# Store queue, start order and weight rows of a gMLP and attention layer

## The chip, the cores and the metric

The kernel runs on one core of one Trainium2 chip. A core has five engines that run at the same time, each with its own list of instructions that it takes in order: TensorE (PE, matmuls and transposes into PSUM), VectorE (DVE), ScalarE (ACT), GpSimd (POOL) and SyncE (SP), which here only issues DMAs. The weight load of a matmul has a row of its own in the profile (PEld). Engines wait for each other through semaphores. The metric is the device time of one execution, in microseconds.

## The reference

One layer over a sequence of 1024 rows with 1024 features, all in float32:

```python
h = rms_norm(x, g_pre)
proj = h @ w_in            # u_A, v_A, z_A, q, k, v_B, z_B, two gates
y_a = spatial_gating(gelu(u_a), gelu(v_a), ln_g, ln_b, w_s, b_s) * silu(z_a)
y_b = mixture_of_dilations(q, k, v_b) * silu(z_b)     # 8 heads of 128
m = g_a * (y_a @ w_pa) + g_b * (y_b @ w_pb)
return x + rms_norm(m @ w_o, g_post)
```

spatial_gating normalises v_A and mixes the 128 rows of each chunk by a 128x128 matrix w_s of each of 16 groups; its bias b_s is added to what w_s makes of ln_b. mixture_of_dilations lets each query see a window of keys at three strides, with a bias that falls with the distance, and combines the three results by their softmax denominators.

## The kernel before

**Products.** Every float32 operand is split in two parts, hi (a rounded copy, made on ScalarE) and lo (the difference, on VectorE or GpSimd); a product is three matmuls: hi by hi, hi by lo and lo by hi. `operand` (L98 to L109) does that for a weight tile and `split` (L159) for an activation.

**Order.** Loops emit the work; a scheduler then sets each engine's list by its own estimate of times and by the order of emission. `tc.issue_after(i)` keeps what is emitted inside it behind instruction i in that order. Pools with few buffers add waits: raw weight tiles and the tiles of y_A share the tag `wr` with three buffers, hi and lo operands have eight each (`wh`, `wl`), PSUM tags have one to three banks. SP issues its DMAs in list order, so a store that waits for its data holds all behind it.

**Start (to 150 us).** Eight row tiles of x are loaded. For each, `norm_tile` squares it on ScalarE (L253), takes the root as a power on GpSimd (L164), scales it by its root and by g_pre on VectorE (L260) and transposes it on TensorE in `transposed` (L241), with the split behind. Meanwhile `warm` (L229) runs idle matmuls. The first weight operands are those of the v_B projection, `vb`, in row pairs. `rows_product` (L148 to L156) runs that projection in passes over eight k; the table in the loop below it names what is emitted ahead of which k (`ahead`): the norm of a further tile, sums of tiles (`sum_tile`), or `spatial_weights(q)` for four groups of w_s. The latter loads w_s, fills two rows of `shift` with a memset (L301) and a DMA, transposes on TensorE (L306), copies and splits, then makes row sums (`wsR`, L313), copies them with VectorE (L314), multiplies them by ln_b and b_s (`wsB`, L318), copies the product and stores it.

**Projections (150 to 1023 us).** All other columns of w_in by a scheme of seven block products. The change leaves them alone.

**Heads (1023 to 1350 us).** `queries_keys` loads q, k (krh, krl) and the distance tables (ta, te, tb) of a head; `residue_values` and `chunk_values` load its values, the latter in 16 small DMAs (L661, L662); `scores` runs the score matmuls (L702 to L704), the add of a table with a row maximum on VectorE (L707) and the exponential on ScalarE (L711); `exchange` (L715 to L724) moves row sums between the patterns, `normalise` (L728 to L742) makes one factor of them, `scale` (L747 to L761) applies it; `weigh` transposes the weights (L779), multiplies them by the values (L798, L813), adds and gates the result (L865, L866) and stores it to o_d (L867). Beside the heads runs the product y_A @ w_pa: `mlp_weights` loads raw tiles of w_pa and yields operands, two tiles of y_A rows (`yf`) at a time come by `mlp_tiles`, and `mlp_products` runs one step of three matmuls (one k) for each `take(steps, 1)`. In names, pa0110 is b 0, m 1, half 1, part 0.

**Tail.** o_d is loaded again, then the products with w_pb (L1046 to L1048) and w_out, the last norm and the output.

## Time and profile before

| | |
|---|---|
| median of 3 runs | 1560.0 us (1558.48 to 1561.28) |
| profiled execution | 1557.3 us |
| its span | 1555.5 us |
| mean granted TensorE clock | 0.991 |
| TensorE busy | 1509.7 us, 97% of the span |
| VectorE, ScalarE, GpSimd busy | 871.0, 683.6, 780.2 us |
| DMA moved | 251.64 MB, 162 GB/s over the span |

The span runs from the first to the last instruction of the profiled execution. A row of a timeline gives start, duration, engine, line, operation, and in brackets how long the engine had been idle before it and what ended that. A row of waits gives who waited for whom: microseconds in all, how many times, the longest. "from issue to landing" is the last number of a DMA row.

### The profile page before, as it was taken

How to read it: one execution, taken by the hardware profiler on the slowest of the kernel's cores; microseconds unless marked ns; L12 is line 12 of the kernel's file. 1: busy time of each engine (PE TensorE's matmuls, PEld its weight loads, DVE VectorE, ACT ScalarE, POOL GpSimd, SP SyncE). 2: the span in 40 equal slices, each digit the busy share in tenths (PEclk: the TensorE clock that was granted, in tenths of full speed). 3: DMA queues.
4: the chain of work that ended last, by engine and by line, in shares of the span. 5: the costliest groups of instructions: out<-in, count | busy, mean ns of one | idle time of the engine just before them, and what ended most of it. 6: DMA issues, size and time to landing. Idle time of an engine off the chain costs nothing.

```text
span 1555.5 us, 22766 instructions
## 1 busy us (share of the span) xinstructions
PE 1509.7 (97%) x7866; PEld 1274.4 (82%) x7866; DVE 871.0 (56%) x1699; ACT 683.6 (44%) x1318; POOL 780.2 (50%) x711
## 2 busy tenths in 40 slices
PE   8999999999999999999999999998999989999998
PEld 5788999988788888788888888877887778878886
...
GB/s 250 158 156 192 140 109 103 107 129 132 171 120 142 135 166 103 164 127 138 154 112 153 105 173 113 128 240 256 202 223 203 224 209 186 247 273 166 185 109 68
DMA packets 247798, 251.64 MB, mean 162 GB/s; under 512 B 14297, under 2 KB 187385, under 8 KB 247426
## 3 DMA queue, kind: packets, MB, share of 16 engines
...
q8 instruction: 62, 1.02, 0.3%
q14 instruction: 54, 0.44, 0.1%
...
HBM read 173.58 MB, written 76.55 MB: 161 GB/s over the span
## 4 chain that ended last, share of the span: by engine, by line
PE 75%; DVE 9%; issue 5%; ACT 4%; DMA 3%; POOL 3%; SPq 0%; POOLq 0%; DVEq 0%; ACTq 0%
PE pa L921 2%; PE pa L922 2%; PE pa L923 2%; PE pb L1047 2%; PE pb L1048 2%; PE pb L1046 2%; PE vb L154 2%; PE vb L155 2%; PE vb L156 2%; PE sg L567 2%; ACT st L711 1%; POOL out L1067 1%; PE pc L813 1%; DVE oth L724 1%; PE pr L798 1%
## 5 line engine op out<-in xcount | busy, mean ns | idle before, releaser
L108 POOL TENSOR_TENSOR wl_pa<-wr_pa,wh_pa 128x512 fp32r<-128x512 f32 x56 | 74.6, 1342 | 42.7 <-ACT wh_pa L106 34.1
L556 DVE TENSOR_SCALAR vn<-vn,mean,rstd 128x128 f32<-128x128 f32 x128 | 58.4, 510 | 35.8 <-DMA vn<-v_d 35.4
L711 ACT ACTIVATE st<-st,own 128x256 f32<-128x256 f32 (+1 forms) x128 | 62.7, 494 | 35.1 <-DVE own L707 35.0
L1046 PE MATMUL pb<-yh,wh_pb 128*128 128x512 f32 x128 | 49.9, 390 | 1.4 <-ACT yh L159 1.4
L106 ACT ACTIVATE wh_pa<-wr_pa 128x512 fp32r<-128x512 f32 x64 | 38.8, 624 | 27.5 <-DMA wr_pa<-in_w_proj_a_dram 18.9
L1047 PE MATMUL pb<-yl,wh_pb 128*128 128x512 f32 x128 | 50.0, 391 | 0.7 <-DVE yl L159 0.5
L1048 PE MATMUL pb<-yh,wl_pb 128*128 128x512 f32 x128 | 49.8, 389 | 0.0
L724 DVE COPY oth<-own 32x4 f32<-32x4 f32 x128 | 36.0, 281 | 15.0 <-ACT st L711 13.4
L1081 ACT ACTIVATE sq<-o 128x512 f32<-128x512 f32 x16 | 9.6, 599 | 74.6 <-PE o L1079 74.6
L159 POOL TENSOR_TENSOR qcl<-q,qch 128x512 fp32r<-128x512 f32 x16 | 27.8, 1739 | 28.1 <-ACT qch L159 28.1
L159 POOL TENSOR_TENSOR vl<-vn,vh 128x512 fp32r<-128x512 f32 x32 | 41.3, 1292 | 0.8 <-ACT vh L159 0.8
L1050 POOL TENSOR_TENSOR mb<-thb,mb 128x512 f32<-128x512 f32 x16 | 20.6, 1289 | 41.7 <-DVE thb L1049 32.2
L724 POOL COPY oth<-own 32x4 f32<-32x4 f32 x128 | 24.0, 188 | 31.6 <-ACT st L711 26.8
L1061 DVE TENSOR_TENSOR sso<-sso 128x1 f32<-128x1 f32 x8 | 1.3, 160 | 67.6 <-ACT sq L1081 67.6
L759 DVE TENSOR_SCALAR st<-st,nm 128x256 f32<-128x256 f32 x64 | 36.9, 619 | 0.3
L164 POOL TENSOR_TENSOR sso<-sso,mhalf 128x1 f32<-128x1 f32 x8 | 4.4, 550 | 59.1 <-DVE sso L163 59.1
L159 DVE TENSOR_TENSOR ptlb<-pb,pthb 128x512 fp32r<-128x512 f32 x32 | 22.0, 688 | 20.2 <-ACT pthb L159 20.2
L866 POOL TENSOR_TENSOR o<-o,zt 128x512 f32<-128x512 f32 x16 | 20.6, 1295 | 24.5 <-DMA zt<-z_d 13.3
L108 POOL TENSOR_TENSOR wl_wos<-wr_wos,wh_wos 128x512 fp32r<-128x512 f32 x16 | 20.7, 1292 | 22.8 <-ACT wh_wos L106 22.8
L707 DVE CUSTOM_DVE_ANT_0 st<-sc,tb 128x256 f32<-128x256 f32 x64 | 23.6, 420 | 14.3 <-PE sc L704 12.9
L779 PE MATMUL pb<-ident,st 128*128 128x128 f32 x128 | 21.2, 286 | 9.5 <-DVE st L759 6.8
L1046 PEld LDWEIGHTS pb<-yh,wh_pb 128*128 128x128 f32 x128 | 24.0, 188 | 6.7 <-ACT yh L159 1.8
...
## 6 DMA issues: line engine op xcount, KB each, us to landing
wr_pa<-in_w_proj_a_dram SPq DMA_DIRECT2D x32, 512.0 KB, 5.7
wr_g<-in_w_in_dram SPq DMA_DIRECT2D x16, 512.0 KB, 3.5
wr_va<-in_w_in_dram SPq DMA_DIRECT2D x16, 512.0 KB, 3.7
wr_u<-in_w_in_dram SPq DMA_DIRECT2D x16, 512.0 KB, 3.7
wr_z<-in_w_in_dram SPq DMA_DIRECT2D x16, 512.0 KB, 3.7
...
wr_yf<-y_d SPq DMA_DIRECT2D x16, 512.0 KB, 5.8
```

What stands on the lines that cost most here:

```text
L106: nc.scalar.activation(hi, src, AF.Copy)
L108: low.tensor_tensor(lo, src, f32(hi), ALU.subtract)
L154: nc.tensor.matmul(ps, lhs[k][0], rh, start=(k == 0), stop=False)
L155: nc.tensor.matmul(ps, lhs[k][0], rl, start=False, stop=False)
L159: return nc.scalar.activation(hi, src, AF.Copy), low.tensor_tensor(lo, src, f32(hi), ALU.subtract)
L556: nc.vector.tensor_scalar(vn[:, c, :], vn[:, c, :], mean[:, 4 * b + c, 0:1], rstd[:, 4 * b + c:4 * b + c + 1], op0=ALU.subtract, op1=ALU.mult)
L711: nc.scalar.activation(st[:, t, :n], st[:, t, :n], AF.Exp, bias=own[:, half, idx, 0:1], scale=-1.0, accum_out=own[:, half, idx, 1:2])
L724: (nc.gpsimd, nc.vector)[half].tensor_copy(dst, src)
L759: nc.vector.tensor_scalar(w, w, f, None, op0=ALU.mult)
L1046: nc.tensor.matmul(ps, lh, rh, start=(k == 0), stop=False)
L1047: nc.tensor.matmul(ps, lh, rl, start=False, stop=False)
L1048: nc.tensor.matmul(ps, ll, rh, start=False, stop=(k == KT - 1))
```

## The change

1. **First rows.** `transposed` also returns the low split, `norm_tile` also the scale. `spatial_weights` is emitted behind tile 0's last transpose and its low split, the first weight operands behind tile 0's scale.
2. **Spatial bias.** The part of `spatial_weights` from wsB on is returned as a function and emitted one step later in the table, behind the newest matmul of `rows_product`.
3. **Stores.** The outputs of the heads go to o_d by GpSimd's queue and no longer by SP's.
4. **Weight rows.** A raw tile of w_pa holds 4 k-blocks of 256 columns (rows of 1 KB) in place of 8 k-blocks of 128 columns. Two such tiles make the operands of two m. There are 32 loads of 512 KB as before.
5. **Chunk values of head 0** are emitted behind `queries_keys(1)` and no longer ahead of head 0's scores.

```diff
@@ -153,7 +153,9 @@
             for ps, lhs in zip(pss, lhss):
                 nc.tensor.matmul(ps, lhs[k][0], rh, start=(k == 0), stop=False)
                 nc.tensor.matmul(ps, lhs[k][0], rl, start=False, stop=False)
-                nc.tensor.matmul(ps, lhs[k][1], rh, start=False, stop=(k == KT - 1))
+                newest[:] = [nc.tensor.matmul(ps, lhs[k][1], rh, start=False, stop=(k == KT - 1))]
+
+    newest = []
 
     def split(hi, lo, src, low=nc.vector):
         return nc.scalar.activation(hi, src, AF.Copy), low.tensor_tensor(lo, src, f32(hi), ALU.subtract)
@@ -239,8 +241,7 @@
             pt = bank("pv", name)
             for k in range(4):
                 last = nc.tensor.transpose(pt[:, k * P:(k + 1) * P], src[:, k * P:(k + 1) * P], ident)
-            split(*[t[:, :, i * P:(i + 1) * P] for t in hl], pt.rearrange("p (k n) -> p k n", k=4))
-            return last
+            return last, split(*[t[:, :, i * P:(i + 1) * P] for t in hl], pt.rearrange("p (k n) -> p k n", k=4))[1]
 
         def norm_tile(c, load=1, between=None):
             b, i = divmod(c, 4)
@@ -257,10 +258,10 @@
             power(ss[:, 1:2], ss[:, 0:1], 1.0 / D)
             for j in range(2):
                 xs = xt[:, 512 * j:512 * (j + 1)]
-                nc.vector.scalar_tensor_tensor(xs, xs, ss[:, 1:2], gpre[:, 512 * j:512 * (j + 1)], op0=ALU.mult,
+                scaled = nc.vector.scalar_tensor_tensor(xs, xs, ss[:, 1:2], gpre[:, 512 * j:512 * (j + 1)], op0=ALU.mult,
                                                op1=ALU.mult)
                 last = transposed(hT[j][b], i, xs, f"xT{c}{j}")
-            return squared, last
+            return squared, scaled, last
 
         def v_out(c, cb, ps):
             if cb:
@@ -312,26 +313,30 @@
             pr_ = bank("sc", f"wsR{q}")
             nc.tensor.matmul(pr_[0:1, :], col, wf, start=True, stop=True)
             nc.vector.tensor_copy(rowsum[0:1, :], pr_[0:1, :])
-            pb = bank("sc", f"wsB{q}")
-            for g in range(4):
-                gs = slice(g * P, (g + 1) * P)
-                nc.tensor.matmul(pb[:, gs], shift[0:2, gs], rowsum[0:2, gs], start=True, stop=True)
-            wb = wpool.tile([P, 512], F32, tag="ws", bufs=2, name=f"wb{q}")
-            nc.scalar.activation(wb, pb, AF.Copy)
-            nc.sync.dma_start(wsb_d[q].rearrange("p g n -> p (g n)"), wb)
+
+            def biases():
+                pb = bank("sc", f"wsB{q}")
+                for g in range(4):
+                    gs = slice(g * P, (g + 1) * P)
+                    nc.tensor.matmul(pb[:, gs], shift[0:2, gs], rowsum[0:2, gs], start=True, stop=True)
+                wb = wpool.tile([P, 512], F32, tag="ws", bufs=2, name=f"wb{q}")
+                nc.scalar.activation(wb, pb, AF.Copy)
+                nc.sync.dma_start(wsb_d[q].rearrange("p g n -> p (g n)"), wb)
+
+            return biases
 
         def norm_weights(squared):
             for j, pg in enumerate(spread):
                 with tc.issue_after(squared.ins):
                     nc.scalar.activation(gpre[:, 512 * j:512 * (j + 1)], pg, AF.Copy)
 
-        squared, turned = norm_tile(0, 0, norm_weights)
+        squared, scaled, turned = norm_tile(0, 0, norm_weights)
         rows = sp.tile([32, P], F32, name="rows")
         wv = []
         for k in range(0, KT, 2):
             if k == 2:
                 norm_tile(4, 0)
-            with tc.issue_after(squared.ins):
+            with tc.issue_after(squared.ins), tc.issue_after(scaled.ins):
                 wv += row_pair(w_in, OFF_VB, k, "vb0", (nc.gpsimd, nc.vector) if k < 4 else (nc.gpsimd, nc.gpsimd))
             if k == 0:
                 load_tile()
@@ -343,14 +348,28 @@
 
         def spatial(q):
             def emit():
-                with tc.issue_after(turned.ins), tc.issue_after(squared.ins):
-                    spatial_weights(q)
+                with tc.issue_after(turned[0].ins), tc.issue_after(turned[1].ins), tc.issue_after(squared.ins):
+                    after[q] = spatial_weights(q)
             return emit
 
+        def bias(q):
+            def emit():
+                with tc.issue_after(newest[0].ins):
+                    after[q]()
+            return emit
+
+        def both(*fs):
+            def emit():
+                for f in fs:
+                    f()
+            return emit
+
+        after = {}
+
         norm, sums = (lambda c, n=1: lambda: norm_tile(c, n)), (lambda i: lambda: sum_tile(i))
-        for cb, cs, tags, ahead in ((0, (0, 4), "mm mm", {1: spatial(0), 2: norm(1), 3: spatial(1), 4: spatial(2), 5: norm(5),
-                                                          6: spatial(3)}),
-                                    (0, (1, 5), "sc sc", {0: norm(2), 2: sums(0), 3: norm(6), 5: sums(1), 6: norm(3), 7: norm(7, 0)}),
+        for cb, cs, tags, ahead in ((0, (0, 4), "mm mm", {1: spatial(0), 2: norm(1), 3: both(bias(0), spatial(1)), 4: both(bias(1), spatial(2)),
+                                                          5: norm(5), 6: both(bias(2), spatial(3))}),
+                                    (0, (1, 5), "sc sc", {0: norm(2), 1: bias(3), 2: sums(0), 3: norm(6), 5: sums(1), 6: norm(3), 7: norm(7, 0)}),
                                     (0, (2, 6, 3, 7), "sc tp mm mm", {3: sums(2)}),
                                     (1, (0, 4, 1, 5), "sc sc sc tp", {3: sums(3)}),
                                     (1, (2, 6, 3, 7), "mm mm sc sc", {})):
@@ -864,7 +883,7 @@
                 o4 = o[:, hs].rearrange("p (a i r) -> p a i r", a=4, r=4)
                 nc.vector.tensor_tensor(o4, po[b].rearrange("p (a r i) -> p a i r", a=4, r=4), o4, ALU.add)
                 nc.gpsimd.tensor_tensor(o[:, hs], o[:, hs], zs[b], ALU.mult)
-                nc.sync.dma_start(o_d[h][:, hs], o[:, hs])
+                nc.gpsimd.dma_start(o_d[h][:, hs], o[:, hs])
             yield
 
 
@@ -888,11 +907,11 @@
 
         def mlp_weights():
             for b, p, half in MLP_ORDER:
-                for m in (2 * p, 2 * p + 1):
-                    raw = raw_tile(w_pa[8 * half * P:8 * (half + 1) * P, m * P:(m + 1) * P].rearrange(
-                        "(k p) n -> p k n", p=P), f"pa{b}{m}{half}")
+                raw = [raw_tile(w_pa[4 * q * P:4 * (q + 1) * P, 2 * p * P:2 * (p + 1) * P].rearrange(
+                    "(k p) n -> p k n", p=P), f"pa{b}{p}{q}") for q in (2 * half, 2 * half + 1)]
+                for m in range(2):
                     for g in range(2):
-                        yield operand(raw[:, 4 * g:4 * g + 4, :], f"pa{b}{m}{half}{g}",
+                        yield operand(raw[g][:, :, m * P:(m + 1) * P], f"pa{b}{2 * p + m}{half}{g}",
                                       nc.vector if (b, p) == (0, 0) else nc.gpsimd)
 
         def mlp_products(ya):
@@ -937,7 +956,6 @@
         take(queries_keys(0, heads[0]))
         take(steps, 8)
         residue_values(0, heads[0])
-        chunk_values(0, heads[0])
         for _ in scores(0, heads[0]):
             take(steps, 1)
         take(exchange(0, heads[0], 0))
@@ -947,6 +965,7 @@
             scale(heads[0], *tile_)
         for _ in queries_keys(1, heads[1]):
             take(steps, 3)
+        chunk_values(0, heads[0])
         before = iter(())
         for h in range(H):
             more = h + 1 < H
```

**What moves at the start.** VectorE, between tile 0's root and the first low split. ss_149 is of tile 0 and ss_187 of tile 4, the second to be worked on; xt_120 is tile 0. Before:

```order
L163 TENSOR_SCALAR ss0_149<-ss0_149,eps_74 128x1
L301 MEMSET shift0_253 2x512
L301 MEMSET shift1_321 2x512
L260 SCALAR_TENSOR_TENSOR xt0_120<-xt0_120,ss0_149,gpre_122 128x512 x2
L108 TENSOR_TENSOR wl_vb0_1_183<-wr_vb0_0_175,wh_vb0_1_181 128x512
L256 TENSOR_TENSOR ss4_187<-ss4_187 128x1
L159 TENSOR_TENSOR hT00l_101<-xT00_159,hT00h_100 128x4x128
L163 TENSOR_SCALAR ss4_187<-ss4_187,eps_74 128x1
```

and now:

```order
L165 TENSOR_SCALAR ss0_149<-ss0_149,eps_74 128x1
L261 SCALAR_TENSOR_TENSOR xt0_120<-xt0_120,ss0_149,gpre_122 128x512 x2
L108 TENSOR_TENSOR wl_vb0_1_183<-wr_vb0_0_175,wh_vb0_1_181 128x512
L257 TENSOR_TENSOR ss4_187<-ss4_187 128x1
L165 TENSOR_SCALAR ss4_187<-ss4_187,eps_74 128x1
L161 TENSOR_TENSOR hT00l_101<-xT00_159,hT00h_100 128x4x128
```

Both memsets of shift have moved behind tile 4's scale, and tile 4's ss stands ahead of hT00l.

TensorE, at the last group of spatial weights (q is 3, the digit behind ws); vb01 are the accumulators of the second pass. Before:

```order
L313 MATMUL wsR3_445<-wf3_428,col_147 1x512
L318 MATMUL wsB3_448<-rowsum3_427,shift3_426 128x128 x4
L154 MATMUL vb01_0_480<-wh_vb0_0_177,hT00h_100 128x512
L155 MATMUL vb01_0_480<-wl_vb0_0_179,hT00h_100 128x512
L156 MATMUL vb01_0_480<-wh_vb0_0_177,hT00l_101 128x512
```

and now:

```order
L314 MATMUL wsR3_445<-wf3_428,col_147 1x512
L154 MATMUL vb01_0_472<-wh_vb0_0_177,hT00h_100 128x512
L155 MATMUL vb01_0_472<-wl_vb0_0_179,hT00h_100 128x512
L156 MATMUL vb01_0_472<-wh_vb0_0_177,hT00l_101 128x512
L154 MATMUL vb01_1_473<-wh_vb0_0_177,hT01h_102 128x512
L155 MATMUL vb01_1_473<-wl_vb0_0_179,hT01h_102 128x512
L156 MATMUL vb01_1_473<-wh_vb0_0_177,hT01l_103 128x512
L154 MATMUL vb01_0_472<-wh_vb0_1_181,hT00h_100 128x512
L155 MATMUL vb01_0_472<-wl_vb0_1_183,hT00h_100 128x512
L321 MATMUL wsB3_505<-rowsum3_427,shift3_426 128x128 x4
```

Eight matmuls of the second pass have come between the row sums and the product that uses them.

**What moves at head 0.** ScalarE, at the exponentials of its scores: st0 are score tiles (st010 of the strided half, st003 of the plain one), wh_pa operand copies of w_pa, ya0201h the copies of the y_A rows that are loaded as yf020 and yf022, qrh1 and qch1 the next head's queries. Before:

```order
L711 ACTIVATE st010_9836,own0_9834<-st010_9836,own0_9834 128x256
L711 ACTIVATE st012_9852,own0_9834<-st012_9852,own0_9834 128x256 x2
L711 ACTIVATE st014_9873,own0_9834<-st014_9873,own0_9834 128x256 x2
L711 ACTIVATE st016_9888,own0_9834<-st016_9888,own0_9834 128x256 x2
L711 ACTIVATE st001_9909,own0_9834<-st001_9909,own0_9834 128x256
L106 ACTIVATE wh_pa0200_9802<-wr_pa020_9800 128x512
L106 ACTIVATE wh_pa0201_9902<-wr_pa020_9800 128x512
L711 ACTIVATE st001_9909,own0_9834<-st001_9909,own0_9834 128x256
L711 ACTIVATE st003_9924,own0_9834<-st003_9924,own0_9834 128x256 x2
L711 ACTIVATE st005_9943,own0_9834<-st005_9943,own0_9834 128x256 x2
L711 ACTIVATE st000_9958,own0_9834<-st000_9958,own0_9834 128x192 x2
```

and now:

```order
L730 ACTIVATE st001_9891,own0_9816<-st001_9891,own0_9816 128x256 x2
L106 ACTIVATE wh_pa0011_9751<-wr_pa003_9745 128x512
L106 ACTIVATE wh_pa0110_9755<-wr_pa002_9743 128x512
L106 ACTIVATE wh_pa0111_9778<-wr_pa003_9745 128x512
L161 ACTIVATE ya0201h_9766<-wr_yf020_9768 128x512 x2
L730 ACTIVATE st003_9906,own0_9816<-st003_9906,own0_9816 128x256 x2
L730 ACTIVATE st005_9925,own0_9816<-st005_9925,own0_9816 128x256 x2
L161 ACTIVATE qrh1_10014<-q10_10020 128x4x128
L161 ACTIVATE qch1_10016<-q10_10020 128x512
L730 ACTIVATE st000_9940,own0_9816<-st000_9940,own0_9816 128x192
L161 ACTIVATE ya0201h_9766<-wr_yf022_9790 128x512 x2
L730 ACTIVATE st000_9940,own0_9816<-st000_9940,own0_9816 128x192
```

The exponentials now stand among copies of four operands and of y_A rows, and the last of them behind the copies of yf022.

**What moves at head 5.** SP, around its keys; ve and va are the values of head 4, ma_d the store of a finished tile of y_A @ w_pa, tha06 its data. Before:

```order
L635 DMA krh5_11829<-k_d_90 128x1024
L113 DMA wr_yf110_11951<-y_d_94 128x2x512
L635 DMA krl5_11830<-k_d_90 128x1024
L639 DMA ta5_12003<-in_alibi_a_dram 128x256
L928 DMA ma_d_95<-tha06_11808 128x512
L639 DMA te5_12005<-in_alibi_e_dram 128x384
L662 DMA ve04_11983<-vb_h_84 16x2x128 x4
L662 DMA ve14_11993<-vb_l_85 16x2x128 x4
L639 DMA tb5_12007<-in_alibi_b_dram 128x384
```

and now:

```order
L654 DMA krh5_11829<-k_d_90 128x1024
L113 DMA wr_yf110_11953<-y_d_94 128x2x512
L947 DMA ma_d_95<-tha06_11808 128x512
L681 DMA ve04_11985<-vb_h_84 16x2x128 x4
L681 DMA ve14_11995<-vb_l_85 16x2x128 x4
L654 DMA krl5_11830<-k_d_90 128x1024
L680 DMA va14_11994<-vb_l_85 32x7x128
L680 DMA va04_11984<-vb_h_84 32x7x128 x4
L680 DMA va14_11994<-vb_l_85 32x7x128 x3
L658 DMA ta5_12005<-in_alibi_a_dram 128x256
L658 DMA te5_12007<-in_alibi_e_dram 128x384
L658 DMA tb5_12009<-in_alibi_b_dram 128x384
```

The low keys have moved behind the store and eight small loads, the tables behind another eight.

## The prediction, made before the result was known

> **What bounds the kernel now.** I read the page's busy times first, then the windows by stage, then the timelines and waits of the stages that are not full.
>
> ```profile
> PE 1509.7 (97%) x7866; PEld 1274.4 (82%) x7866; DVE 871.0 (56%) x1699; ACT 683.6 (44%) x1318; POOL 780.2 (50%) x711
> 0.00:20.00 20.00, 15.85 (x43) 7.65 (x43) 9.80 (x21) 10.10 (x21) 7.64 (x12) 1.00 0.64 224
> 20.00:40.00 20.00, 19.48 (x98) 12.74 (x99) 13.71 (x28) 13.89 (x32) 4.55 (x6) 1.00 0.90 276
> 40.00:60.00 20.00, 17.23 (x90) 13.15 (x90) 13.84 (x25) 10.03 (x24) 7.56 (x7) 0.91 0.58 186
> 500.00:600.00 100.00, 100.00 (x456) 82.92 (x455) 63.08 (x97) 39.23 (x64) 54.48 (x41) 1.00 0.44 140
> 1025.00:1060.00 35.00, 28.70 (x140) 22.71 (x139) 25.07 (x80) 24.51 (x59) 18.59 (x28) 0.87 0.84 240
> 1235.00:1265.00 30.00, 24.44 (x137) 19.71 (x136) 17.74 (x32) 12.36 (x25) 15.90 (x11) 1.00 0.70 213
> ```
>
> The columns of a window are its length, the busy time of PE, PEld, DVE, ACT and POOL with instruction counts, the granted clock, the DMA share and GB/s. TensorE is the bound: 1509.7 of 1555.5 us, and in the projections (500 to 600) it has no hole, so nothing done there can pay. Its 45.8 us of holes lie at the ends and among the heads: 4.1 us before 20, 2.8 us from 40 to 60 at a clock of 0.91, 6.3 us from 1025 to 1060 at 0.87, 5.6 us from 1235 to 1265. The change touches exactly those windows.
>
> **The first rows.** The timeline of the start:
>
> ```profile
> 7.43 0.55 POOL L164 TENSOR_TENSOR ss<-ss,mhalf 128x1 f32<-128x1 f32 x1 [6.14 <-DVE ss L163]
> 7.87 0.60 ACT L326 ACTIVATE gpre<-gpre 128x512 f32<-128x512 f32 x1
> 8.59 2.34 PE L229 MATMUL warm<-idle 128*128 128x512 bf16 x5
> 11.10 0.48 DVE L301 MEMSET shift<- 2x512 f32 x1 [2.61 <-PE warm L229]
> 11.51 1.91 DVE L260 SCALAR_TENSOR_TENSOR xt<-xt,ss,gpre 128x512 f32<-128x512 f32 x2
> 12.81 1.97 PE L241 MATMUL xT<-ident,xt 128*128 128x128 f32 x8 [1.88 <-DVE xt L260]
> 15.20 0.20 DVE L163 TENSOR_SCALAR ss<-ss,eps 128x1 f32<-128x1 f32 x1
> 15.49 0.93 POOL L164 TENSOR_TENSOR ss<-ss,mhalf 128x1 f32<-128x1 f32 x1 [3.28 <-DVE ss L163]
> 16.52 3.38 DVE L260 SCALAR_TENSOR_TENSOR xt<-xt,ss,gpre 128x512 f32<-128x512 f32 x2
> 20.05 0.63 PE L241 MATMUL xT<-ident,xt 128*128 128x128 f32 x4 [0.88 <-DVE xt L260]
> ```
>
> The scale of tile 0 has its root at 7.98 and its whole weight row at 8.47, but stands on VectorE behind a memset that waits for the warm-up matmuls to give back a buffer. In the new order of VectorE, shown with the change, both memsets have gone behind the second tile's scale, and the second tile's ss (ss4) ahead of the first low split. Now the scale starts at 7.98 and its first half ends near 8.9 (half of 1.91). The transposes then wait for PE itself, whose warm-up ends at 10.93: 1.88 us earlier than 12.81. For the second tile the power on POOL no longer waits until 15.20: it follows POOL's own work and can run some 3 us earlier, and with it the scale of 16.52 and the 0.88 us hole at 20.05. So the lead is between 1.9 (the transposes alone) and 3.1 us. The spatial weights' loads go one place back on SP and their transposes behind the second tile's, where PE has no stall now. Below stands nothing gained: from 20 to 40 the DMA share is 0.90, and a PE that arrives early may find the later tiles missing; against it, PE is 19.48 of 20 busy there. I take -2.5, range 0 to -3.1.
>
> **The bias later.** The timeline at 41 us:
>
> ```profile
> 41.27 1.02 PE L313 MATMUL wsR<-wf,col 128*1 128x512 f32 x2
> 43.95 0.67 DVE L314 COPY rowsum<-wsR 1x512 f32<-1x512 f32 x1
> 44.67 1.15 PE L318 MATMUL wsB<-rowsum,shift 2*128 2x128 f32 x8 [2.39 <-DVE rowsum L314]
> 47.02 0.43 PE L156 MATMUL vb<-wh_vb,hT01l 128*128 128x512 f32 x1
> 47.25 0.63 PE L154 MATMUL vb<-wh_vb,hT00h 128*128 128x512 f32 x1
> 47.68 0.63 PE L155 MATMUL vb<-wl_vb,hT00h 128*128 128x512 f32 x1
> PE wsB L318 <- DVE rowsum L314: 2.5, 2, 2.4
> ```
>
> PE makes the last row sum, and its next instruction needs that sum back from VectorE. In the new order eight matmuls of 0.23 us (47.02 to 47.25) lie in the hole: 1.8 of its 2.39 us. Behind the old hole six matmuls start 0.43 apart (47.25 to 47.68) instead of 0.23: 6 x 0.20 = 1.2 us at half speed, which should go with the hole. I take -3.0, range -1.8 to -3.6. The other waits of this kind were short (2.5 us in all, of which this one is 2.4).
> The Trainium skill says the same of the slow stretch (TensorE: Matmul & The Clock Gate, "What's actually happening"): the array falls to half its clock after an idle window of about 3.4 us that runs on its own time. By that rule a hole of 0.6 us could still meet such a window and nothing but the 1.8 would be gained; the trace shows the slow run starting 2.6 us behind the hole's end.
>
> **Head 0: values later, wide weight rows.** Waits, timeline and loads at the first head:
>
> ```profile
> 1026.58 0.32 SPq L516 DMA_DIRECT2D th_d<-g14u  x1
> 1042.91 1.15 ACT L106 ACTIVATE wh_pa<-wr_pa 128x512 fp32r<-128x512 f32 x2 [0.94 <-DMA wr_pa<-in_w_proj_a_dram]
> 1046.87 0.44 ACT L711 ACTIVATE st<-st,own 128x192 f32<-128x192 f32 x1
> 1047.31 1.09 ACT L159 ACTIVATE qrh<-q 128x512 fp32r<-128x512 f32 x1
> 1046.06 2.83 DVE L724 COPY oth<-own 32x4 f32<-32x4 f32 x16 [3.35 <-ACT st L711]
> 1053.31 1.39 PE L779 MATMUL pb<-ident,st 128*128 128x128 f32 x4 [5.06 <-DVE st L759]
> wr_pa<-in_w_proj_a_dram SPq DMA_DIRECT2D x32, 512.0 KB, 5.7
> wr_z<-in_w_in_dram SPq DMA_DIRECT2D x16, 512.0 KB, 3.7
> wr_yf<-y_d SPq DMA_DIRECT2D x16, 512.0 KB, 5.8
> 1033.90 0.69 DVE L108 TENSOR_TENSOR wl_pa<-wr_pa,wh_pa 128x512 fp32r<-128x512 f32 x1
> ```
>
> PE idles 5.06 us for the first scaled tile of head 0. ScalarE's exponentials set that: they end with the last of 0.44 behind 1046.87, VectorE exchanges (1046.06, 2.83 us) and normalises, and the tile comes at 1053.31. So what the change does here is read from when those exponentials end. In the new ScalarE order (shown with the change) six of eight score pairs come early on PE, but their exponentials stand in a row with the operand copies of the wide raw tiles, and the last one behind the copies of the second half of tile yf02 (wr_yf022). That tile is at the end of a chain through the three raw buffers, since a wide raw serves both m in turn and is held until the third or fourth of four operands: pa001 goes out behind the store of 1026.58, at 1026.9; pa003 takes pa000's buffer once its second operand is copied, two copies (1.15) and a VectorE split (0.69) behind pa001's landing; yf022 takes pa002's buffer, two copies and a split (1.9) behind pa003's. With 5.7 us a landing: 1032.6, then 1034.5 to 1040.2, then 1042.1 and yf's 5.8, 1047.9; two copies and the exponential give 1049.5, 2.2 later than before's 1047.3. With the 3.7 of the loads from w_in, which have 1 KB rows already but met emptier engines, it is 1030.6, 1036.2, 1043.9, and then ScalarE's own work behind 1036.2 decides: seven copies of 0.58, two of q's of 1.09 and six exponentials of 0.44 to 0.5, 9.2 in all, end at 1045.4, 1.9 earlier. TensorE's holes on the way are no extra, since in both orders the same instructions stand ahead of that first tile. I take +0.5, between the two. Range -3.3 (the 1.9, and the 0.94 and half of a copy pair that ScalarE lost at 1042.91 out of the way) to +5 (both loads as late as the 0.84 DMA share of this window may make them, one more landing time at 5.7 in all, beside the clock of 0.87). The sixteen chunk loads go behind that traffic; their first use comes some 30 us later.
>
> **Head 5: the order on SP.** Further down the low keys and bias tables of head 5 have moved behind head 4's values, and the keys behind a store for which SP waits. Their times before:
>
> ```profile
> 1189.86 0.97 SPq L635 DMA_DIRECT2D krl<-k_d  x1
> 1198.53 0.32 SPq L928 DMA_DIRECT2D ma_d<-tha  x1
> 1203.12 0.42 SPq L639 DMA_DIRECT2D tb<-in_alibi_b_dram  x1
> krl<-k_d SPq DMA_DIRECT2D x8, 512.0 KB, 8.1
> 1202.04 0.41 PE L702 MATMUL sc<-krh,qrh 128*128 128x256 f32 x1
> ```
>
> Keys go out at about 1203 instead of 1189.86 and land (8.1) at 1211; PE took them at 1202.04, so head 5's scores come 9 us late. PE has MLP steps to fill with, and the new order does so. Before, head 6 has this displacement, and its window (1235 to 1265) lost 5.6 us; in the new order head 6's two key loads stand side by side. So -5.6 to +9; as one head loses what the other gains, I take 0.
>
> **Stores on GpSimd, 1 KB rows.** Rows of the stores:
>
> ```profile
> L867 SPq DMA_DIRECT2D o_d<-o x16: 319/350/1470, 1100.4 to 1349.9; - x16
> L866 POOL TENSOR_TENSOR o<-o,zt x16: 1282/1297/1301, 1096.5 to 1348.6; 128x512 f32<-128x512 f32 x16
> ```
>
> No DMA issued by POOL is in this trace; the nearest rows are SP's 0.35 us per issue and POOL's own 1.3 us operation. So 16 stores cost POOL 5.6 to 20.8 us, over 250 us in which it is half idle, and SP is rid of 5.6 us. I take 0 to TensorE, range -2 to +2. Weight loads keep their number and bytes; with rows twice as long I take -0.5, range -2 to 0.
> A rule of the Trainium skill speaks against it (SBUF — State Buffer, "SBUF: two separate sides"): a transfer that GpSimd issues waits while a VectorE operation of a two-port mode holds the port they share, and its example grows from 0.62 to 3.1 us. By it each store lands up to 2.5 us later, an estimate; nobody reads them before the tail, so the sum would grow by 2.5 at most, at the last store. No run here shows it yet.
>
> **The sum.** -2.5 - 3.0 + 0.5 + 0 + 0 - 0.5 = -5.5 on the profiled execution's 1557.3 (1555.5 and 1.8 around it): 1551.8. The median of the runs shown is 2.7 above that execution, so 1554.5.
>
> **Rivals.**
> (a) The start's gain is spent in the heads or never arrives: the 0.90 DMA share leaves only the bias hole's -3.0, and head 0 takes 2.2 of it: 1559.2, no change that can be told. For it: the chain of three loads above. Against: the bias hole needs no transfer.
> (b) Slower. SP serves in order, and head 5's keys behind the store that waits leave PE without scores for the full 9 us, and head 0 costs 2.2, while the start gives 5.5: 1560 - 5.5 + 9 + 2.2 = 1565.7. It decides when the hole at head 5 passes the start's 5.5. Against: MLP steps stand in between.
> (c) More: head 0 at its good end (-3.3) and head 6 with 3 us of its 5.6 back: 1560 - 5.5 - 3.3 - 3 = 1548.2.
> (d) The stores tie up POOL, at 1.3 us each with the low splits and scales behind them; a quarter of the 20.8 us exposed is +5 on the forecast: 1559.7.
>
> **How the numbers follow.** What a measurement here can tell from no change is about 0.2%, 3.1 us: faster is under 1556.9. Forecast 0.46 (its own range 1551.5 to 1557.5, of which 0.04 is no change), (a) 0.19, (b) 0.14, (c) 0.15, (d) 0.06. Faster is 0.42 and (c), 0.57; same 0.04, (a) and (d), 0.29; slower (b), 0.14. The range holds the forecast, (a), (d) and half of (c): 1548.5 to 1562.0.
>
> **What would show it.** Right: no memset ahead of the first scale and transposes at about 10.9; no wait of wsB on rowsum over 1 us and a clock near 1.00 from 40 to 60; in head 0 ScalarE's copy of yf022 waiting for its load just ahead of the last exponential, and pb's first tile within 3 us of its old place relative to the start. Wrong: that tile 5 us late; scores of head 5 with PE idle ahead of them; POOL-issued stores of over 1.3 us each with PE waiting on GpSimd's low splits. The forecast falls if the first 150 us do not end 4 us earlier.

## The result and the profile after

| | before | changed |
|---|---|---|
| median | 1559.2 us (4 runs, 1557.5 to 1561.3) | 1575.2 us (4 runs, 1572.9 to 1577.9) |
| profiled execution, span | 1555.5 us | 1572.4 us |
| mean granted TensorE clock | 0.991 | 0.982 |

The ratio is 1.0102, with an interval of 1.0081 to 1.0124: the change is **slower by 1%**, where 1554.5 us had been forecast, 1548.5 to 1562.0. The profile after, busy times and windows:

```profile
PE 1516.0 (96%) x7866; PEld 1280.4 (81%) x7866; DVE 872.3 (55%) x1699; ACT 684.4 (44%) x1318; POOL 788.0 (50%) x727
40.00:60.00 20.00, 17.64 (x102) 13.82 (x102) 18.61 (x31) 10.92 (x24) 7.61 (x6) 1.00 0.55 176
1080.00:1100.00 20.00, 15.68 (x82) 13.46 (x81) 13.58 (x29) 8.19 (x13) 13.07 (x10) 0.83 0.82 260
1160.00:1180.00 20.00, 16.90 (x88) 14.60 (x87) 13.66 (x30) 10.01 (x20) 11.22 (x10) 0.83 0.72 227
```

The same two windows among the heads before:

```profile
1080.00:1100.00 20.00, 18.80 (x113) 15.57 (x111) 18.54 (x43) 10.94 (x21) 12.44 (x10) 1.00 0.77 226
1160.00:1180.00 20.00, 19.50 (x124) 17.03 (x124) 13.74 (x44) 11.76 (x35) 12.76 (x25) 1.00 0.87 215
```

The span grew by 16.9 us with the same 7866 matmuls: 10.6 are more holes of TensorE (1572.4 - 1516.0 = 56.4 against 45.8), 6.3 are matmuls that ran longer; in the two windows among the heads the granted clock is 0.83, where it was 1.00. From 500 to 600, in the projections, TensorE is busy throughout, as before. The two windows among the heads, for which the prediction had no term, hold over a quarter fewer matmuls than before (82 for 113, 88 for 124).

Where the 16.9 us arise is read best by asking when each kernel has done the same amount of TensorE work. I added up the matmuls of each trace by width (0.227 us for 512 columns, 0.119 for 256, 0.11 for less, the starting distances in the full-speed stretches; warm-up left out), and compared the times at which the sums are equal. Each row is one profiled execution against the one before; negative is ahead. Differences in the text were taken before rounding.

```
time in before        30    80   150  1000  1060  1080  1180  1240  1340  1400
start_only          -1.5  -3.9  -2.7  -3.0  -0.3  -0.2  -0.2  -0.1  -0.3  -0.2
the whole change    -1.7  -4.2  -3.3  -4.3  -3.3  -2.5  +8.0 +10.9 +13.1 +16.8
start_chunk         -1.5  -3.8  -2.9  -2.8  -4.9  -3.8  -1.2  +6.4  +4.1  +5.7
start_pairs         -2.3  -5.0  -3.8  -5.1  -2.3  -1.0  -1.0  -2.1  +7.9 +12.7
start_stores        -1.4  -3.9  -2.8  -3.8  -4.9  -5.0  -8.1  +1.8  -4.4  -0.1
stores_last_on_sync -2.4  -5.0  -3.7  -4.9  -5.6  -5.8  -9.0  +1.6  -4.5  -3.2
all_but_chunk       -1.5  -4.2  -3.0  -4.2  +0.1  +1.9  -1.6  +9.4  +4.3  +8.7
all_but_pairs       -2.2  -4.5  -3.3  -4.2  -5.0  -5.5  +2.5  +5.2  +8.3 +12.5
all_queries_held    -1.5  -4.0  -2.6  -3.9  -2.3  -1.4  +3.8  +6.7  +8.6 +12.0
pairs_keys_first    -1.7  -4.1  -3.2  -4.4  -1.3  +0.2  -0.6  +0.6  +3.1  +6.7
best_keys_first     -1.5  -4.1  -2.7  -4.1  -5.2  -4.9  -6.7  +3.7  -3.8  -1.4
keys_first_whole    -3.2  -5.8  -4.7  -6.0  -5.5  -4.7  +6.6  +8.4  +3.9  +9.2
last_on_sync_whole  -1.8  -4.1  -3.2  -4.1  -3.0  -2.2  +7.0 +11.2 +12.0 +14.0
whole_mended        -2.3  -4.1  -2.8  -4.0  -2.6  -1.8  +2.1  +3.2  -3.9  -4.3
mended_without_4_5  -1.7  -3.9  -2.8  -3.7  -1.8  -1.6  -2.7  +7.0  +2.9  +4.4
```

The names are those of the experiments below. A row shows where a kernel loses; what it costs is read from the medians, since one execution can stand apart from them (start_only and start_stores end level here, and their medians are 2.7 us apart). The whole change arrives at the heads 4.3 us ahead, loses 1.8 to 1080, **10.5 from 1080 to 1180**, 5.1 from there to 1340 and 3.8 at the tail.

**The head turns.** A turn is where one head's last scores and the next head's transposes meet. ScalarE's timeline at the turn behind head 0, after:

```profile
1086.50 0.63 ACT L106 ACTIVATE wh_pa<-wr_pa 128x512 fp32r<-128x512 f32 x1 [4.51 <-DMA wr_pa<-in_w_proj_a_dram]
1087.04 0.58 ACT L161 ACTIVATE ptha<-pa 128x512 fp32r<-128x512 f32 x1
1089.04 1.11 ACT L161 ACTIVATE qrh<-q 128x512 fp32r<-128x512 f32 x1
1090.05 1.11 ACT L161 ACTIVATE qch<-q 128x512 fp32r<-128x512 f32 x1
1091.06 1.11 ACT L161 ACTIVATE qrh<-q 128x512 fp32r<-128x512 f32 x1
1092.06 1.11 ACT L161 ACTIVATE qch<-q 128x512 fp32r<-128x512 f32 x1
1093.07 0.36 ACT L161 ACTIVATE ptha<-pa 128x256 fp32r<-128x256 f32 x1
1094.19 0.41 DVE L161 TENSOR_TENSOR ptla<-pa,ptha 128x256 fp32r<-128x256 f32 x1
1094.65 1.11 PE L798 MATMUL pb<-ident,st 128*128 128x128 f32 x4 [4.32 <-DVE ptla L161]
```

Before, at the same turn:

```profile
1085.86 1.17 ACT L159 ACTIVATE qch<-q 128x512 fp32r<-128x512 f32 x1
1086.90 0.40 ACT L159 ACTIVATE pthe<-pe 64x256 fp32r<-64x256 f32 x1
1090.98 0.58 ACT L159 ACTIVATE ptha<-pa 128x512 fp32r<-128x512 f32 x1
1091.98 0.37 ACT L159 ACTIVATE ptha<-pa 128x256 fp32r<-128x256 f32 x1
```

ptha is the copy of the transposed weights out of PSUM; TensorE's next transposes (pb) wait until its low half ptla is made. Before, the query copies of the coming head (qrh, qch) ended ahead of pthe. After, four of them, 4.0 us from 1089.04 to 1093.07, stand between the two halves of ptha (1087.04 and 1093.07). TensorE idles 4.32 us, and the granted clock of that window is 0.83.

The copies are not the whole of this hole. Ahead of the first half ScalarE had waited 4.51 us for a raw tile of w_pa, a load that edit 4 changes. start_chunk and all_but_pairs, below, have edit 5 and the narrow raw tiles; in both the four copies stand ahead of ptha at this turn, no such wait precedes them, and the hole is 1.09 and 1.70 us. So at this turn edits 4 and 5 act together. The waits from 1000 to 1360 of the whole change show how often pb waits:

```profile
PE pb L798 <- DVE ptla L161: 10.7, 5, 4.3
```

Before, in the heads:

```profile
PE pb L779 <- DVE ptla L159: 2.6, 1, 2.6
```

**The tables.** SP's list in the heads, after (the last chunk loads ahead of head 5's low keys, and the tables tb of heads 5 and 6):

```profile
1208.54 2.27 SPq L681 DMA_DIRECT2D ve<-vb_l  x4
1217.49 0.36 SPq L658 DMA_DIRECT2D tb<-in_alibi_b_dram  x1
1260.62 0.43 SPq L658 DMA_DIRECT2D tb<-in_alibi_b_dram  x1
```

The table of head 5 went out at 1203.12 before. It now goes out 14 us later, behind sixteen chunk loads of the head ahead; 8 us of that are the lag that the kernel has at 1180 in any case. The tables of heads 6 and 7 stand behind sixteen and eight. The kernel before has some of this already (eight ahead of the table tb of head 5 and the tables of head 7, sixteen ahead of low keys and tables of head 6).

**The tail.** The last head's output, after, with the load that needs it:

```profile
1361.60 1.30 POOL L885 TENSOR_TENSOR o<-o,zt 128x512 f32<-128x512 f32 x1 [1.97 <-DVE o L884]
1362.86 1.29 POOL L108 TENSOR_TENSOR wl_pa<-wr_pa,wh_pa 128x512 fp32r<-128x512 f32 x1
1364.09 0.58 POOL L886 DMA_DIRECT2D o_d<-o  x1
1369.07 0.97 SPq L1011 DMA_DIRECT2D yf<-o_d  x2
o_d<-o POOLq DMA_DIRECT2D x16, 256.0 KB, 4.1
```

The same before:

```profile
1349.88 0.32 SPq L867 DMA_DIRECT2D o_d<-o  x1
1351.99 0.93 SPq L992 DMA_DIRECT2D yf<-o_d  x2
o_d<-o SPq DMA_DIRECT2D x16, 256.0 KB, 2.2
```

From the end of the gating (1361.60 and 1.30) to the load of the heads' output it is now 6.2 us, before 2.1 (1349.88 is its end): 1.2 us because a low split of weights stands ahead of the store in GpSimd's list, 2.9 because the load follows the issue of the store by 5.0 us and no longer by 2.1. The trace has this store's landing 4.8 us behind its issue. The two medians above are of sixteen landings after and of the five that the trace has before.

### The profile page after: what moved, and what is told of

Its sections match the earlier page's. It is cut to its first block, busy times and chain, and to the rows that moved or that the text cites. A ratio compares the mean times of both kernels' runs of the same rounds, so it can differ in the third digit from the quotient of the medians.

```text
span 1572.4 us, 22771 instructions
## 1 busy us (share of the span) xinstructions
PE 1516.0 (96%) x7866; PEld 1280.4 (81%) x7866; DVE 872.3 (55%) x1699; ACT 684.4 (44%) x1318; POOL 788.0 (50%) x727
## 4 chain that ended last, share of the span: by engine, by line
PE 74%; DVE 7%; DMA 6%; issue 5%; ACT 3%; POOL 3%; SPq 1%; ACTq 0%; POOLq 0%; DVEq 0%
PE pa L941 2%; PE pa L942 2%; PE pa L940 2%; PE pb L1066 2%; PE pb L1067 2%; PE pb L1065 2%; PE vb L156 2%; PE sg L586 2%; PE vb L154 2%; PE vb L155 2%; DMA wr_yf<-y_d 1%; POOL out L1086 1%; PE pr L817 1%; DMA vn<-v_d 1%; DMA krl<-k_d 1%
## 5 line engine op out<-in xcount | busy, mean ns | idle before, releaser
L798 PE MATMUL pb<-ident,st 128*128 128x128 f32 x128 | 23.9, 301 | 17.1 <-DVE ptla L161 10.7
L778 DVE TENSOR_SCALAR st<-st,nm 128x256 f32<-128x256 f32 x64 | 40.2, 670 | 0.3
L743 DVE COPY oth<-own 32x4 f32<-32x4 f32 x128 | 31.3, 244 | 13.1 <-ACT st L730 11.4
L798 PEld LDWEIGHTS pb<-ident,st 128*128 128x128 f32 x128 | 16.9, 152 | 24.4 <-DVE ptla L161 12.8
L161 ACT ACTIVATE pthb<-pb 128x512 fp32r<-128x512 f32 x32 | 18.9, 591 | 41.0 <-PE pb L798 40.9
```

The lines of the kernel that those rows point to most:

```text
L161: return nc.scalar.activation(hi, src, AF.Copy), low.tensor_tensor(lo, src, f32(hi), ALU.subtract)
L743: (nc.gpsimd, nc.vector)[half].tensor_copy(dst, src)
L778: nc.vector.tensor_scalar(w, w, f, None, op0=ALU.mult)
L798: nc.tensor.transpose(pt[:n, c0:c0 + P], src, ident)
```

## The experiments

Three causes were on trial. A: moving the chunk values puts the four query copies ahead of the transposed weights' copies on ScalarE. B: the pairs of wide raw tiles hold two of the three raw buffers, so loads go out late. C: the stores on GpSimd end the heads later. The rival to each was that another of the three carries the loss, or that the start's gain itself shifts the heads into it.

Each kernel is the kernel before with some of the five edits, or the whole change with one thing altered. The kernel before was timed beside each group of them, at 1558.1 to 1559.7.

### One edit at a time

start_only is edits 1 and 2; against the whole change:

```diff
-                nc.gpsimd.dma_start(o_d[h][:, hs], o[:, hs])
+                nc.sync.dma_start(o_d[h][:, hs], o[:, hs])
...
-                raw = [raw_tile(... 4 k-blocks of 256 columns ...) for q in (2 * half, 2 * half + 1)]
+                for m in (2 * p, 2 * p + 1):
+                    raw = raw_tile(... 8 k-blocks of 128 columns ...)
...
         residue_values(0, heads[0])
+        chunk_values(0, heads[0])
         for _ in scores(0, heads[0]):
...
-        chunk_values(0, heads[0])
         before = iter(())
```

start_chunk, start_pairs and start_stores leave one of the three pieces as in the change: edit 5, edit 4, edit 3.

> Only the two edits of the start (first rows, bias); heads as before. All theories: the start gives 4.2 us (the lag between the two traces at equal work is -4.2 at 60 us), the heads are those of before: 1559.2 - 4.2 = 1555. If the start's lead is lost on the way (that would be the forecast's rival a), 1559.

> The start's edits and the chunk values of head 0 behind the next head's queries. Theory A (this edit alone moves the four query copies ahead of the transposed chunk weights on ScalarE at the first three heads, 4.4 us of copies each, of which the holes 4.48, 1.49 and 3.26 us show): 1555 + 9 to 11 = 1564 to 1566. Theory B (the paired raw tiles) and theory C (GpSimd's stores): as the start alone, 1555.

> The start's edits and the raw tiles of w_pa in pairs with 1 KB rows. Theory B (a pair holds two of three raw buffers, its loads come late and ScalarE's list stands behind them): 1555 + 13 = 1568. Theory A: 1553 to 1558, head 0 alone may differ. Theory C: 1555.

> The start's edits and the stores by GpSimd. Theory C (the issue of 0.58 us on GpSimd and landings of 4.1 instead of 2.2 us delay the heads): 1555 + 17 = 1572. Theories A and B: only the tail pays, where the last store's landing is awaited, +3.7: 1559.

Measured, with the kernel before at 1558.1: start_only 1555.9 (ratio 0.9981, 0.9970 to 0.9992), start_chunk 1566.3 (1.0051, 1.0031 to 1.0072), start_pairs 1570.8 (1.0077, 1.0058 to 1.0096), start_stores 1558.6 (1.0001, 0.9989 to 1.0014). The start helps, by 2.2 us, and each of the three other edits costs on top of it: edit 5 10.4 us, edit 4 14.9, edit 3 2.7 (the intervals of start_only and start_stores just meet). Edit 5 alone has the head turn's wait, though it loses at other turns than the whole change: 2.6 us from 1080 to 1180 and 7.6 from there to 1240, where the longest hole, 5.5 us, stands behind head 3. In the waits from 1065 to 1360 of start_chunk:

```profile
PE pb L798 <- DVE ptla L161: 10.2, 4, 5.5
```

Edit 4 alone loses at three other places (lead of start_pairs): 4.1 us from 1000 to 1080, at head 0, 10.0 from 1240 to 1340, and 4.8 at the tail. At the second, SP issues head 7's low keys behind the chunk loads, and the engines that make its scores run dry. The low keys and a window of start_pairs:

```profile
1292.63 0.42 SPq L654 DMA_DIRECT2D krl<-k_d  x1
1296.00:1301.00 5.00, 5.00 (x29) 4.24 (x28) 0.00 (x0) 0.00 (x0) 1.25 (x1) 1.00 0.99 330
```

In start_only these low keys went out ahead of the chunk loads, at 1275.17. VectorE and ScalarE do nothing for 5 us; TensorE spends its MLP steps there and lacks them later. Edit 3 alone gains 4.2 us among the first heads (lead from 3.8 to 8.1 between 1000 and 1180); at 1340 its lead is 4.4, where start_only has 0.3 left, and it loses these 4.4 at the tail.

### One edit left out

all_but_chunk is the whole change without edit 5, all_but_pairs without edit 4 (the pieces of the diff above).

> The whole change without the move of the chunk values. Theory A (that move puts four query copies ahead of the transposed chunk weights on ScalarE at the first head turns): the 10.5 us that the change loses between 1080 and 1180 come back, 1575 - 10.5 = 1564.5. Theory B (the pairs of raw tiles alone cost the heads): 1571 or more, since the pairs are still there.

> The whole change with the narrow raw tiles of before. Theory A: about as the start with the chunk move, 1566. Theory B: the 15 us that the pairs added to the start come back, 1575 - 15 = 1560.

Measured, with the kernel before at 1559.0: 1565.7 (1.0043, 1.0026 to 1.0059) and 1569.6 (1.0065, 1.0051 to 1.0080). Taking edit 5 out gives 9.5 us, as theory A had it; taking edit 4 out gives 5.6, and both expectations there (1566 and 1560) missed. The effects do not add: on the start edit 4 cost 14.9, in the whole change it costs 5.6. Nor does the wait of pb need edit 5: all_but_chunk loses nothing from 1080 to 1180, but 11 us from there to 1240, where pb waits 6.84 us for ptla at the turn behind head 4, with a wait of 3.52 us for w_pa and four query copies ahead of the second ptha on ScalarE. So the price belongs to the order that comes out in the end, not to an edit by itself, and the next kernels alter that order directly.

### The order on ScalarE, and the last stores

all_queries_held is the whole change with the queries' split copies kept behind the newest split of transposed weights (`parts`), which also needed the queries of the head after to be taken later:

```diff
+                with ExitStack() as after_:
+                    for i_ in parts:
+                        after_.enter_context(tc.issue_after(i_.ins))
-                split(*[w[:, :, b * P:(b + 1) * P] for w in res["qr"]], ...)
+                    split(*[w[:, :, b * P:(b + 1) * P] for w in res["qr"]], ...)
...
-                if i > 4:
+                if i > 8:
                     take(ahead, 1)
```

stores_last_on_sync is start_stores with the last head's two stores on SP:

```diff
-                nc.gpsimd.dma_start(o_d[h][:, hs], o[:, hs])
+                (nc.sync if h == H - 1 else nc.gpsimd).dma_start(o_d[h][:, hs], o[:, hs])
```

> The whole change, but the split copies of the queries of head h+2 are emitted behind, and kept behind, the last transposed chunk weights of head h. If ScalarE's order is what costs at the head turns (theory A): the waits of pb on ptla shrink from 10.7 us to under 4 and the time falls by 5 to 10, to 1565 to 1570. If the chunk move costs by its loads on SP's queue instead: 1573 to 1577.

> The start's edits and the stores by GpSimd, but the last head's two stores issued by SP as before. Theory C's tail (the last store lands 2 us later and stands behind a low split on GpSimd): the 4.4 us lost at 1360 to 1380 come back, 1558.6 - 4 = 1554.5. If the tail is late for another reason: 1558.6.

Measured, with the kernel before at 1559.0: all_queries_held 1567.7 (1.0051, 1.0035 to 1.0067), 7.5 us under the whole change, as theory A had it; from 1080 to 1180 it loses 5.2 where the whole change lost 10.5. The waits of pb on ptla shrink as expected, from 10.7 us (from 1000 to 1360):

```profile
PE pb L801 <- DVE ptla L161: 2.4, 1, 2.4
```

So about half of the head turns' loss goes with the copies' order on ScalarE. What is left up to 1180 holds three holes of 0.9 to 1.0 us, two of them for low keys, and a granted clock of 0.87 from 1080 to 1100.

stores_last_on_sync 1554.8 (0.9974, 0.9964 to 0.9984): with the last two stores back on SP the 4.4 us of the tail shrink to 1.3, and the kernel is faster than the kernel before and than start_stores. It is not told apart from start_only, whose interval (0.9970 to 0.9992) overlaps its own. It has neither edit 4 nor edit 5, and still a turn of the same kind:

```profile
1237.42 1.09 PE L798 MATMUL pb<-ident,st 128*128 128x128 f32 x4 [6.48 <-DVE ptla L161]
```

On ScalarE four query copies and four of y_A stand there between the two halves of ptha (1227.14 and 1235.17). start_only has no such hole there, so an order of this kind can come out of edit 3 as well.

### The order on SP

pairs_keys_first is start_pairs, best_keys_first is stores_last_on_sync, each with this edit:

```diff
                     for tile_ in TILES[1]:
                         scale(heads[h + 1], *tile_)
-                    chunk_values(h + 1, heads[h + 1])
                 if i > 4:
                     take(ahead, 1)
             take(ahead)
+            if more:
+                chunk_values(h + 1, heads[h + 1])
```

whole_mended is the whole change with all three edits: queries held, keys first, last stores on SP.

> Edits 1, 2 and 4 as in start_pairs, but the chunk values of the next head are emitted behind its queries, keys and tables, so that at every head but the first SP has the low keys and tables ahead of the sixteen value loads. The copies on ScalarE keep their order through the first five heads. Theory (the pairs' cost lies in two places: 4.4 us at head 0, where the raw tiles come late, and 9.9 us between 1240 and 1340, where head 7's low keys stand behind the value loads): 1570.8 - 9.9 = 1561, between 1559 and 1564; head 0 loses its 4.4 us as before, and head 7's low keys go out some 15 us earlier. Rival (the pairs hold two of three raw buffers at every step, and the late keys only show it): at least 1568, the loss moving to other weight loads.

> The whole change with three mends: the queries' split copies behind the transposed weights' copies (as in all_queries_held, 1567.7), the chunk values behind the next head's keys and tables, the last head's two stores on SP. If the three are all that the change loses besides head 0: 1567.7 - 4 for the tail = 1563.7, and less by 3 to 6 for the keys of heads 5 and 7: 1558 to 1561. Rival (each fix moves the order elsewhere, as the single edits did): 1563 to 1569.

> stores_last_on_sync (1554.8) with the chunk values behind the next head's keys and tables. In the trace of stores_last_on_sync the lead over the kernel before falls from 9.0 us at 1180 to 2.7 at 1260, where head 6's low keys stand behind eight value loads and its tables behind sixteen. Theory (late keys): half of that or more returns, 1550 to 1553. Rival (the loss is the new order of steps, not the keys, or the values come late now): 1554 to 1558.

Measured, with the kernel before at 1558.7: pairs_keys_first 1564.6 (1.0037, 1.0023 to 1.0051), 6.1 us under start_pairs, a little short of the expected 7 to 12. Head 7's low keys and the window that was empty:

```profile
1277.00 0.73 SPq L654 DMA_DIRECT2D krl<-k_d  x1
1296.00:1301.00 5.00, 5.00 (x39) 4.56 (x37) 3.20 (x11) 3.99 (x13) 1.61 (x3) 1.00 0.11 43
```

The keys are 15.6 us earlier and both engines work; from 1240 to 1340 it loses 2.5 us, where start_pairs loses 10.0, and the 4.6 us at head 0 stay, as expected. At the turn behind head 5 the edit also moves the query copies on ScalarE behind both halves of ptha, so the share of the keys alone is not shown. whole_mended 1556.4 (0.9987, 0.9971 to 1.0003): 18.8 us under the whole change, better than the 1558 to 1561 expected, and not told apart from the kernel before. best_keys_first 1555.4 (0.9974, 0.9964 to 0.9984): no gain over stores_last_on_sync, so the theory that its late keys cost 2 to 4 us fell; the wait of pb on ptla is still there, 6.04 us at 1239.

mended_without_4_5 is whole_mended without edits 4 and 5.

> whole_mended without edits 4 and 5: edits 1, 2 and 3, and the three mends (queries' split copies behind the transposed weights' copies, chunk values behind the next head's keys and tables, last head's stores on SP). Head 0 then has the old weight rows and the old place of the values, which was worth 2.6 us at 1060 (lead 5.2 in best_keys_first against 2.6 in whole_mended). Theory (edits 4 and 5 only cost, the mends keep): 1556.4 - 2.6 = 1554, between 1551 and 1555. If the mends gain only together with edits 4 and 5: 1556 or more, at best what best_keys_first has without the held queries, 1555.4.

Measured 1558.6, with the kernel before at 1558.8 (1.0000, 0.9990 to 1.0011). The theory (1551 to 1555) fell, and the other reading held, by which the mends gain only together with edits 4 and 5 (1556 or more). TensorE's and SP's timelines of mended_without_4_5 show the new wait:

```profile
1235.95 0.37 SPq L113 DMA_DIRECT2D wr_pa<-in_w_proj_a_dram  x1
1237.52 0.38 SPq L657 DMA_DIRECT2D krh<-k_d  x1
1244.88 0.55 PE L724 MATMUL sc<-krh,qrh 128*128 128x256 f32 x1 [6.65 <-DMA krh<-k_d]
```

Head 6's keys stand behind a weight load for which SP waits, and TensorE idles 6.65 us for them. In whole_mended they go out 2.9 us later still (1240.44) and no hole of TensorE over 1.5 us follows up to the tail. The same rules on another base give another list; why one has other work at that place was not taken further.

### Each mend alone on the whole change

keys_first_whole and last_on_sync_whole are the whole change with the edit of pairs_keys_first, and with that of stores_last_on_sync.

> The whole change with the chunk values of the next head behind the keys and tables of the head after. In the whole change the tables of heads 2, 3, 5, 6 and 7 stand behind 8 or 16 value loads in SP's list, here none does from head 2 on. If the three mends add up: whole_mended 1556.4 is 11.3 below all_queries_held; 3.8 of it is the tail, 7.5 the keys: 1575.2 - 7.5 = 1567.7, between 1564 and 1571. If they only act together: 1572 or more.

> The whole change with the last head's two stores on SP; ScalarE's copies and SP's loads keep their order through the heads. If the tail adds up: 1575.2 - 3.8 (start_stores 1558.6 against stores_last_on_sync 1554.8) = 1571.4, between 1570 and 1573, the yf loads of the tail going out about 2 us behind the last gating and no longer 6.2. If something else holds the tail: 1574 or more.

Measured, with the kernel before at 1559.7: 1568.1 (1.0069, 1.0049 to 1.0089) and 1570.9 (1.0082, 1.0066 to 1.0098), both as expected if the mends add. The table of head 6 in keys_first_whole:

```profile
1247.78 0.44 SPq L658 DMA_DIRECT2D tb<-in_alibi_b_dram  x1
```

It goes out 12.8 us earlier than in the whole change (1260.62), those of heads 5 and 7 by 11 and 9. Its turns up to 1180 cost the same (11.3 us from 1080), but from 1180 to 1340 it gains 2.7 where the whole change loses 5.1. The edit also moves query copies on ScalarE at the turns of heads 4 to 6, so a part of this may be ScalarE's; how large a part was not separated. The tail of last_on_sync_whole:

```profile
1360.52 1.30 POOL L885 TENSOR_TENSOR o<-o,zt 128x512 f32<-128x512 f32 x1 [2.14 <-DVE o L884]
1361.84 0.32 SPq L886 DMA_DIRECT2D o_d<-o  x1
1364.05 0.88 SPq L1011 DMA_DIRECT2D yf<-o_d  x2
```

2.2 us from the gating's end to the load, as before. On the whole change the three mends are worth 7.5, 7.1 and 4.3 us, 18.9 in all, and together they brought 18.8: here they add. By the ratios, which take out the drift of the kernel before between the groups, it is 0.0051, 0.0033 and 0.0020, 0.0104 of the 0.0115 that the three bring together, within the intervals.

## Why the prediction was wrong

**In the terms of its sum.** The lead of the whole change gives -4.3 us at the first head (said -5.5 for first rows and bias), +1.8 at head 0 (+0.5), +10.5 at the head turns (no term), +5.1 at heads 5 to 7 (0) and +3.8 at the tail (0): +16.8, by the medians +16.0.

**The step that failed: a move costed at nothing.** "The sixteen chunk loads go behind that traffic; their first use comes some 30 us later." Fifteen of them go out from 1059.87 to 1071.21, their first use is at 1080.52, and TensorE does not wait for them, so that is not the cost. But with these loads emitted later, ScalarE's order changes at the turns of heads 0, 1 and 2, where four query copies of 1.0 us come ahead of the last weights' copy. The order had been read at the first head and at head 5 and not at the turns between, and no term of the sum stood there. On the start the move costs 10.4 us (start_chunk); in the whole change, leaving it out gives 9.5 and holding the copies back gives 7.5. At the turn with the longest hole the late raw tiles of edit 4 share in it, as shown above.

**First rows, -2.5 said.** Right: 1.4 to 2.4 us ahead at 30 in most executions (3.2 in one), within the range 0 to 3.1. Transposes, the sum's wait and a later hole, after:

```profile
9.57 1.32 PE L243 MATMUL xT<-ident,xt 128*128 128x128 f32 x8 [1.84 <-DVE xt L261]
42.61 1.15 PE L321 MATMUL wsB<-rowsum,shift 2*128 2x128 f32 x8 [0.68 <-DVE rowsum L315]
49.30 0.63 PE L243 MATMUL t2T<-ident,t2f 128*128 128x128 f32 x4 [1.69 <-DVE t3l L161]
```

No memset stands ahead of the scale. The transposes began at 9.57, not 10.9, since in this execution the warm-up ended earlier; in start_only they began at 10.73.

**Bias, -3.0 said.** Right in size, at its lower part: 2.5 us from 30 to 80. The wait is 0.68 us (under 1 as said), and the clock from 40 to 60 is 1.00 for 0.91 in this execution. But the slow stretch does not always go with the hole. In three of the fifteen profiled executions that have this edit (last_on_sync_whole, mended_without_4_5 and all_but_pairs) the clock is half for 3.4 us from 45 us on, behind a hole of 0.7. last_on_sync_whole:

```profile
42.65 1.15 PE L321 MATMUL wsB<-rowsum,shift 2*128 2x128 f32 x8 [0.71 <-DVE rowsum L315]
40.00:60.00 20.00, 19.23 (x102) 15.20 (x103) 18.61 (x31) 11.02 (x24) 7.61 (x6) 0.91 0.54 175
```

The Trainium skill's rule (TensorE: Matmul & The Clock Gate, "What's actually happening"), by which a hole of 0.6 us could still meet a slow window, agrees with these three. They gain as much, 2.2 to 2.3 us from 30 to 80: the other twelve have a new hole of 1.4 to 1.7 us at 49, where a transpose of summed tiles waits for VectorE's low split (t3l), and the three do not. The prediction had no term for this second wait. The lead at 150 is 3.3, not 4: by the sign given, the forecast was to fall, though the shortfall there is only 0.9 us, a wait for a low weight split on GpSimd near 144 that the kernel before did not have.

**The start's sum.** Of the 5.5 us said for both, start_only keeps 2.2 at the end, by the medians. Its profiled execution, the slowest of its eleven, has 3.0 us of lead at 1000 and 0.3 at 1060, so rival (a), the gain spent at head 0, holds for most of it. With the whole change the lead outlives head 0 and is lost later.

**Head 0, +0.5 said.** The mechanism was right, the size off: +1.8 from 1000 to 1080. ScalarE and TensorE's waits from 1025 to 1060, after:

```profile
1041.14 1.14 ACT L161 ACTIVATE ya0201h<-wr_yf 128x512 fp32r<-128x512 f32 x2
1042.18 0.45 ACT L730 ACTIVATE st<-st,own 128x192 f32<-128x192 f32 x1
PE pa L941 <- DVE ya0201l L161: 2.8, 1, 2.8
PE pa L940 <- ACT ya0201h L161: 2.8, 1, 2.8
```

The last exponential does stand behind the copy of that tile of y_A, and the 5.06 us hole ahead of pb has shrunk to 0.84. But "TensorE's holes on the way are no extra" was wrong: TensorE's list needs the tile's products first, and two holes of 2.8 us replace the one. Without edit 5 this head costs 4.1 (start_pairs) and 6.1 (all_but_chunk), at and over the +5 of the range.

**Head 5, 0 said.** The mechanism was there and the value was not 0. It was wrong to let one head's loss stand against another's gain: the stretch from 1180 to 1340, in which heads 5, 6 and 7 have late tables, loses 5.1 us, and with keys and tables first it gains 2.7 on the kernel before (keys_first_whole, 7.1 us in all, a part of it perhaps ScalarE's). Rival (b), slower by keys that come late, was the right direction; it had one head and 9 us, 1565.7 in all, and nothing of the turns and the tail.

**Stores, 0 said.** Two effects hide in that 0: on the start they bring 4.1 us more lead than start_only has at 1340, and lose 4.4 at the tail. Rival (d) is out: an issue takes GpSimd 0.58 us (the row at 1364.09), not 1.3. The Trainium skill's rule (SBUF — State Buffer, "SBUF: two separate sides") gave up to 2.5 us at the last store, and the stores do land 1.9 us later (4.1 for 2.2, the medians above). But the cause it names cannot be the cause at the end: VectorE there runs nothing. The tail of keys_first_whole shows it:

```profile
1354.90 0.58 POOL L886 DMA_DIRECT2D o_d<-o  x1
1360.93 0.88 SPq L1012 DMA_DIRECT2D yf<-o_d  x2
1365.87 0.69 DVE L161 TENSOR_TENSOR yl<-yf,yh 128x512 fp32r<-128x512 f32 x1 [12.84 <-DMA yf<-o_d]
```

VectorE is idle from 1353.0 to 1365.9, and the store issued at 1354.90 still frees the load only at 1360.93. In the six executions whose last store GpSimd issues, the load follows that issue by 5.0 to 6.0 us, with the DMA engines 0.76 to 0.82 busy in between. In the ten with SyncE it follows by 2.1 to 2.8 us (once at a DMA share of 1.09), but by 4.5 in start_pairs at a share of 0.95; so busy DMA engines can delay a store, and do not explain all six. The Trainium skill (DMA: Bandwidth & Descriptors, "Specifications") gives about 1 us to the first byte on GpSimd's path and 0.6 on SyncE's; the medians here are 1.9 apart, so that is not the whole of it. That GpSimd's list had a weight split ahead of the store (1.2 us) was not in the prediction at all.

**1 KB rows, -0.5 said.** Wrong in sign. The loads of w_pa land in 6.5 us, before 5.7, and the two tiles that must be present at once move the loads behind them. What the width of the rows does by itself was not isolated; edit 4 as a whole costs 5.6 to 14.9 us, depending on the rest, and with the three mends edits 4 and 5 together cost nothing (1556.4 with them, 1558.6 without).

**What stays open.** Why moving loads by themselves makes the scheduler place the query copies there was not tried. Why the stores' move brings some 4 us among the heads was not separated from the order that comes with it, nor were late keys and tables from the query copies that move with them. More buffers for the raw weight tiles, which would test the pairs' part at head 0 directly, were not tried.
